# Column sums of all eighth pairs ahead of the second slice, weights rounded later in a block, keys turned one tile later, in a one-core hybrid attention and mLSTM layer

## The chip, the cores and the metric

The kernel runs on one core of a Trainium2 chip. The core's engines work from queues of their own: PE (TensorE, matmuls), DVE (VectorE), ACT (ScalarE), POOL (GpSimd) and SP (SyncE, which here only issues transfers). An instruction waits at the head of its engine's queue until what it needs is there, and what stands behind it in that queue waits too. The metric is device time in microseconds (us); before the change the median of three runs is 1348.02.

## The reference

One layer over 2048 tokens of width 1024, all in float32:

```python
mod = c_act @ w_ada[l] + b_ada[l]
shift, scale, gate = jnp.split(mod, 3, axis=-1)
h = rmsnorm(h_res, norm_w[l]) * (1.0 + scale[:, None, :]) + shift[:, None, :]
y = hybrid_mixer(h, w_in[l], b_in[l], conv_w[l], conv_b[l], rpb[l], ml_norm_w[l], w_out[l])
h_res = h_res + gate[:, None, :] * y
...
def hybrid_mixer(h, w_in, b_in, conv_w, conv_b, rpb, ml_norm_w, w_out):
    proj = h @ w_in + b_in
...
    na_out = neighbourhood_attention(na_q, na_k, na_v, rpb) * jax.nn.silu(na_z)
    qk = jax.nn.silu(centred_short_conv(jnp.concatenate([ml_q, ml_k], axis=-1), conv_w, conv_b))
...
    h_fwd = mlstm_chunkwise(mq, mk, mv, i_f, f_f)
    h_bwd = flip(mlstm_chunkwise(flip(mq), flip(mk), flip(mv), flip(i_b), flip(f_b)))
    hm = (h_fwd + h_bwd).transpose(0, 2, 1, 3) * jax.nn.sigmoid(ml_o).reshape(B, T, ML_HEADS, ML_HEAD_DIM)
...
    return jnp.concatenate([na_out, ml_out], axis=-1) @ w_out
```

`c_act` is silu of the conditioning vector. `proj` is 1024 columns to 4624: queries, keys, values and gate of an attention with 8 heads over a grid of 32 x 64 tokens, the same and one more for an mLSTM with 4 heads that runs in both directions, and 16 columns of mLSTM gates. `centred_short_conv` is a convolution with five taps along the tokens. The last step is another RMSNorm.

## The kernel before

Every float32 matmul of the projection is done in three passes with operands split in a high and a low part: high by high, high by low, low by high. So the 1024 rows that are summed over, eight k-tiles of 128, make 24 matmuls for a tile of output. Each part of the weights has therefore to be "rounded" once it is loaded: ACT copies it to its high half `whi`, another engine subtracts that from the raw weights into the low half `wlo`. `raw_w` (L201) issues the two loads of a block of 256 columns, 512 KB each (`raw0`, `raw1`, one buffer each), and hands back two functions, `parts`, which round a half each when they are called. There are two slots for rounded weights, `wslot` (`_a` and `_b` in the trace), used in turn by even and odd blocks.

Tokens are worked in four groups of 512. `hhi` and `hlo` are the halves of h, turned so that k runs over the partitions, for a group. PSUM is used as four buffers `pp` for results, three `tp` for transposes, and one bank `sp` for everything small.

**The start** (`start`, L218) runs with its instructions in the order in which they are written. The modulation is a sum over eight k-tiles of `w_ada`, loaded in 32 transfers of 256 KB in the order in which they are used. It is worked out for an eighth of the columns of h at a time, two eighths (a pair, `e` from 0 to 3) together. `opened(e)` begins the pair's sum in the `sp` bank with the bias. A k-tile of the table `direct` is added on PE by matmuls one column wide; all others are added up on DVE in `acc` (`summed`, L272). `total(e)` (L283) adds `acc` on PE with a column of ones, and `columns(e)` (L286) has ACT make the scale and shift columns `gT` and `shT` of it. `first_h(k)` (L303) then has ACT write `hhi` and h from the turned x, and hands back the subtraction `hlo` for DVE; the list `early` holds two such subtractions. `vo_first` (L589) is a generator: each `next(first)` issues one slice, that is k-tile k of block 0 for the first four token tiles, 8 matmuls with `hhi` (L598) and 4 with `hlo` (L601). `turned(k)` has PE turn x of k into a `tp` bank, two or three slices ahead. The loop over `e` has two slices in each step; `finish()` in it makes total and columns of the next pair.

**Blocks 0 to 5** are values and output gates, tiles of 128 tokens by 256 columns, 24 matmuls each (`mm3`, L541, lines 544 to 546). `vo_group` and `nav_group` do a group of four tiles: a PSUM buffer each, 24 matmuls, and the eviction by DVE, an addition of the bias into `stvo` or `stv` (L618). `tok_blocks` (L676) goes over blocks 2 to 5 and has the next block's two halves rounded behind groups 0 and 1, with the low half on DVE. From here on the order is set by a scheduler at build time, which goes by estimated costs and by what each instruction depends on; `behind` (L1105) is a dependency of order alone, without a wait. After each tile the loops pull one step of `self.chain`, the mLSTM's gate chain (`gate_chain`, L699): the gates are turned on PE into the `sp` bank, `ps_gi` and then `ps_gf`, DVE copies each out to `wide` (L722, L723), then come Exp, Ln, scans, and the table of decays.

**Blocks 6 to 9** are keys and queries of the mLSTM (`conv_blocks`, L869), with columns on the partitions: tiles `pc` of 128 columns by 512 tokens, 24 matmuls each, in four `pp` buffers. ACT evicts a tile with its bias to `u` (L891, four buffers). `conv_step` then advances all tiles under way by one step of `conv_group` (L917), so that a `yield` in it is one tile later: first nothing, then five taps on DVE into `acc_k` or `acc_q` (four buffers) and a SiLU on ACT (L929), then a store to `d_ck`, and for keys one step later four transposes on PE into `kt` (L939), an eviction `stk` on ACT (L941) and a store.

After that come the queries and keys of the attention (`pq`, L986), the mLSTM's two passes, the attention and the output projection; the change does not touch them.

Of the kernel before, what the change touches and what calls it, by code (L numbers as in the profile page):

```python
# [8 lines left out]
F32 = mybir.dt.float32  # L9
F32R = mybir.dt.float32r  # L10
AF = mybir.ActivationFunctionType
ALU = mybir.AluOpType
# [3 lines left out]
P = 128  # L16
# [4 lines left out]
GT = 512  # L21
# [41 lines left out]
class Kernel:  # L63
# [137 lines left out]
    def raw_w(self, blk, slot, halves=(0, 1)):  # L201
        nc = self.nc
        hi, lo = self.wslot[slot]

        def part(half):
            raw = self.raw.tile([P, 4, 256], F32, tag=f"raw{half}", name=f"raw_{blk}_{half}")
            nc.sync.dma_start(raw, self.w_main[blk, :, 4 * half : 4 * half + 4, :])
            ks = slice(4 * half, 4 * half + 4)

            def run(eng=nc.gpsimd):  # L210
                nc.scalar.activation(hi[:, ks, :256], raw, AF.Copy)
                eng.tensor_tensor(lo[:, ks, :256], raw, hi[:, ks, :256].bitcast(F32), ALU.subtract)

            return run

        return [part(half) for half in halves]

    def start(self, left):  # L218
        nc = self.nc
# [41 lines left out]
        def added(e, left, right):  # L261
            for j in range(4):
                left_tile = left[:, j // 2, (j % 2) * P : (j % 2 + 1) * P]
                groups[e] -= 1
                nc.tensor.matmul(mods[e][:, j : j + 1], left_tile, right, start=False, stop=groups[e] == 0)
# [6 lines left out]
        def summed(e, kt):  # L272
            w, c = sums.pop((e, kt)), cact[:, kt : kt + 1]
            if kt in direct[e]:
                added(e, w, c)
            elif kt == 0:
                acc[e] = ada.tile([P, 2, 256], F32, tag="acc", bufs=2, name=f"acc_{e}")
                nc.vector.tensor_scalar(acc[e], w, c, None, ALU.mult)
            else:
                nc.vector.scalar_tensor_tensor(acc[e], w, c, acc[e], ALU.mult, ALU.add)  # L280
            next(stream, None)

        def total(e):  # L283
            added(e, acc.pop(e), self.ones[:, 0:1])

        def columns(e):  # L286
            ks, ps = slice(2 * e, 2 * e + 2), mods.pop(e)
            for j in range(2):
                k = slice(2 * e + j, 2 * e + j + 1)
                nc.scalar.activation(self.gT[:, k], ps[:, 2 + j : 3 + j], AF.Identity, bias=nw[:, k], scale=nw[:, k])  # L290
            nc.scalar.activation(self.shT[:, ks], ps[:, 0:2], AF.Copy)

        direct = {0: (1, 3), 1: (1,), 2: (1,), 3: (1,)}
        sums, acc, groups = {}, {}, {}
        tps, mods = {}, {}

        def turned(k, tts=(0, 1, 2, 3)):
            if k not in tps:
                tps[k] = self.tp.tile([P, GT], F32, tag="tp", name=f"tp_0_{k}")
            for tt in tts:  # L300
                nc.tensor.transpose(tps[k][:, tt * P : (tt + 1) * P], xt[tt][:, k * P : (k + 1) * P], self.ident)

        def first_h(k):  # L303
            hi = self.hhi[0][:, k, :]
            tp = tps.pop(k)
            h = xp.tile([P, GT], F32, tag="h", bufs=2, name=f"h_0_{k}")
            for dst in (hi, h):
                nc.scalar.activation(dst, tp, AF.Identity, bias=self.shT[:, k : k + 1], scale=self.gT[:, k : k + 1])
            return lambda: nc.vector.tensor_tensor(self.hlo[0][:, k, :], h, hi.bitcast(F32), ALU.subtract)
# [14 lines left out]
        raws = []  # L324
# [22 lines left out]
        hi, lo = self.wslot[0]  # L347
# [34 lines left out]
        for e in range(4):  # L382
            k = 2 * e
            rest = [kt for kt in range(KT) if e < 3 and kt not in direct[e + 1]]
            early = [first_h(k), first_h(k + 1)]
            for n, kt in enumerate(rest[:5]):
                summed(e + 1, kt)
                if n in (2, 4):
                    early.pop(0)()
            for fn in early:  # L390
                fn()
            if e == 1:
                raws[1](nc.vector)
            for kt in rest[5:]:
                summed(e + 1, kt)
            if e == 2:
                for _ in stream:
                    pass
                parts = self.raw_w(1, 1)
                nc.sync.dma_start(self.bgate, self.b_row[0:1, 1536:1552].broadcast_to([P, 16]))  # L400
                self.load_bias(0)
                self.load_bias(1)
                parts[0](nc.vector)

            def finish():
                total(e + 1)
                columns(e + 1)

            next(first)
            if k + 3 < KT:  # L410
                turned(k + 3)
            if e < 3:
                opened(e + 1)
                summed(e + 1, direct[e + 1][0])
            if e == 0:
                finish()
            next(first)
            if k + 4 < KT:
                turned(k + 4)
            if e in (1, 2):  # L420
                finish()
        for tt in range(4, 8):
            load_x(tt)
        parts[1]()
# [147 lines left out]
    def nav_group(self, blk, slot, g):  # L572
        nc = self.nc
        c0 = (blk - 4) * 256
        st = self.stage_tile(f"stv_{blk}_{g}")
        for o in range(4):
            ps = self.pp.tile([P, GT], F32, tag="pp", name=f"pv_{blk}_{g}_{o}")
            self.tok_tile(ps[:, :256], self.wslot[slot], 4 * g + o)
            nc.vector.tensor_add(st[:, o, :256], ps[:, :256], self.brows[blk % 2])
            next(self.chain, None)  # L580
            if o == 1:
                self.flush()
        dst = self.d_vna[g * GT : (g + 1) * GT, c0 : c0 + 256].rearrange("(o p) c -> p o c", p=P)
        self.defer(lambda: nc.sync.dma_start(dst, st[:, :, :256]))
# [91 lines left out]
    def tok_blocks(self, chain_pool):  # L676
        self.wide = chain_pool.tile([P, 2 * D], F32, name="wide")
        self.chain = itertools.chain(self.gate_both(chain_pool), self.decays(chain_pool))
        order = [2, 3, 4, 5]
        next(self.chain)  # L680
        self.tables_begin(chain_pool)
        for n, blk in enumerate(order):
            parts = self.raw_w(blk + 1, (blk + 1) % 2)
            if blk < 5:
                self.load_bias(blk + 1)
            for g in range(NG):
                if blk < 4:
                    self.vo_group(blk, blk % 2, g)
                else:
                    self.nav_group(blk, blk % 2, g)  # L690
                if g < 2:
                    parts[g](self.nc.vector)
            if n > 0:
                self.tables_columns(n - 1)
        for _ in self.chain:
            pass
        self.flush()
# [219 lines left out]
    def conv_group(self, pool, u, kind, ct, g):  # L917

        nc = self.nc
        yield  # L920
        acc = pool.tile([P, GT], F32, tag="acc", bufs=4, name=f"acc_{kind}_{ct}_{g}")
        cc = ct + (0 if kind == "q" else 4)
        for j in range(5):
            src, w = u[:, j : GT + j], self.cw[:, cc, j : j + 1]
            if j == 0:
                nc.vector.tensor_scalar(acc, src, w, None, ALU.mult)
            else:
                nc.vector.scalar_tensor_tensor(acc, src, w, acc, ALU.mult, ALU.add)
        nc.scalar.activation(acc, acc, AF.Silu, bias=self.cb[:, cc : cc + 1])  # L929
        yield  # L930
        j = 0 if kind == "q" else 1
        dst = self.d_ck[ct, 4 * g : 4 * g + 4, :, 385 + j * CH : 385 + (j + 1) * CH].rearrange("c p t -> p c t")
        nc.sync.dma_start(dst, acc.rearrange("p (c t) -> p c t", t=CH))
        yield
        if kind == "q":
            return
        ps = self.tp.tile([P, GT], F32, tag="tp", name=f"kt_{ct}_{g}")
        for o in range(4):
            nc.tensor.transpose(ps[:, o * P : (o + 1) * P], acc[:, o * CH : (o + 1) * CH], self.ident)  # L939
        st = self.stage_tile(f"stk_{ct}_{g}")[:, :, 0:128]  # L940
        nc.scalar.activation(st, ps.rearrange("p (a q) -> p a q", a=4), AF.Copy, scale=KSCALE)  # L941
        d2 = self.d_ck[ct, 4 * g : 4 * g + 4, :, 0:128].rearrange("o p c -> p o c")
        nc.sync.dma_start(d2, st)
# [872 lines left out]
```

## Time and profile before

| | before |
|---|---|
| three runs, us | 1343.64, 1349.42, 1348.02 (median 1348.02) |
| profiled execution, us | 1342.71, of which its span 1340.9 |
| data moved | 255.91 MB, 191 GB/s on the mean |
| start up to the last slice of the first four tiles | 0 to 54 us |
| block 2 begins; key and query blocks | 148 us; 342 to 532 us |
| share of `pq` (L986) in the chain that ended last | 21% |

The profile is of one execution. Its page names groups of instructions by line, engine and tile, output first: `pvo<-whi_a,hhi` is a matmul from `whi_a` and `hhi` into the PSUM tile `pvo`. Behind `<-` in square brackets stands the idle time of the engine before the instruction, and what ended it. In a row of waits the three numbers are the total in us, how many there were, and the longest. In windows each engine has its busy time and, in brackets, its instructions; the granted clock is the share of full speed at which TensorE was allowed to run. Matmuls are pipelined, so the length of one overlaps the next, and the distance between two starts tells more of the pace. The mean granted clock over the whole span is 0.988.

### The profile page before, as it was taken

To read this page: it belongs to the slowest core of one execution; us is meant where nothing else is said; L and a number is where in the kernel's file an instruction comes from. 1 tells how busy PE (TensorE), PEld (TensorE's weight loads), DVE (VectorE), ACT (ScalarE), POOL (GpSimd) and SP (SyncE) were. 2 spreads that over 40 slices of the span, in tenths; PEclk is the share of its full clock that TensorE was granted. 3 is DMA by queue.
4 is the path that set the end of the run, shared out by engine and by line. 5 is a ranking of instruction groups with operands and counts; after the bars stand their busy time and mean duration, and the time that the engine had idled before them with its cause. 6 is when DMAs were issued, how large, how long until landed. Compare 5 with 4: busy or idle time off the path is not lost.

```text
span 1340.9 us, 23409 instructions
## 1 busy us (share of the span) xinstructions
PE 1302.3 (97%) x8330; PEld 1121.7 (84%) x8330; DVE 779.5 (58%) x2404; ACT 543.1 (40%) x1184; POOL 227.0 (17%) x281
## 2 busy tenths in 40 slices
PE   9899899999999999999999999999999999999996
PEld 8899899999877787888888888888877777778785
DVE  5654342212444769256677777777547676766664
ACT  5443323643223423123333323333346555565551
POOL 0144102341000000001212002212202211212221
PEclk8899899999999999999999999999999999999998
DMA  9997545997337775535656867655788987868871
GB/s 321 307 256 182 182 134 156 219 255 217 95 88 216 172 193 163 177 111 141 192 175 191 244 193 212 217 177 169 207 254 226 217 194 189 188 180 192 197 185 48
DMA packets 240486, 255.91 MB, mean 191 GB/s; under 512 B 31078, under 2 KB 200294, under 8 KB 240370
## 3 DMA queue, kind: packets, MB, share of 16 engines
q1 hardware_dynamic: 157006, 182.98, 48.9%
q0 software_dynamic: 20496, 36.21, 11.2%
q10 hardware_dynamic: 62868, 35.22, 9.2%
q8 instruction: 66, 1.08, 0.3%
q14 instruction: 50, 0.41, 0.1%
HBM read 169.81 MB, written 92.72 MB: 196 GB/s over the span
## 4 chain that ended last, share of the span: by engine, by line
PE 48%; DMA 7%; DVE 5%; issue 4%; ACT 2%; POOL 1%; ACTq 0%; SPq 0%; DVEq 0%; POOLq 0%
PE pq L986 21%; PE y L1565 9%; DMA tab<-d_t 4%; PE pT L1505 3%; PE pO L1520 2%; PE pS L1477 2%; PE px L1225 2%; PE pi L1227 2%; PE pc L544 2%; PE pc L546 2%; PE pc L545 2%; PE dc L1165 1%; DMA ck<-d_ck 1%; PE a L1212 1%; DVE pbuf L1485 1%
## 5 line engine op out<-in xcount | busy, mean ns | idle before, releaser
L986 PE MATMUL pq<-hhi,whi_a 128*128 128x512 f32 x512 | 208.2, 407 | 0.8 <-ACT u L891 0.8
L986 PE MATMUL pq<-hlo,whi_a 128*128 128x512 f32 x512 | 208.4, 407 | 0.0
L986 PE MATMUL pq<-hhi,wlo_a 128*128 128x512 f32 x512 | 206.6, 404 | 0.0
L986 PEld LDWEIGHTS pq<-hhi,whi_a 128*128 128x128 f32 x512 | 96.8, 189 | 17.7 <-ACT u L891 1.2
L986 PEld LDWEIGHTS pq<-hhi,wlo_a 128*128 128x128 f32 x512 | 96.8, 189 | 16.4
L986 PEld LDWEIGHTS pq<-hlo,whi_a 128*128 128x128 f32 x512 | 96.7, 189 | 16.0 <-issue 0.5
L1507 ACT ACTIVATE pt<-pT 96x384 f32<-96x384 f32 (+3 forms) x128 | 65.9, 515 | 86.0 <-PE pT L1505 83.4
L960 POOL TENSOR_TENSOR wlo_a<-rawq,whi_a 128x1024 fp32r<-128x1024 f32 x20 | 48.2, 2411 | 306.1 <-ACT whi_a L959 292.7
L1486 ACT ACTIVATE pbuf<-pbuf,mn 128x480 f32<-128x480 f32 (+5 forms) x128 | 76.1, 595 | 51.8 <-DVE mn L1485 49.1
L1565 PE MATMUL y<-hhi,whi_a 128*128 128x512 f32 x256 | 91.6, 420 | 0.5 <-ACT whi_a L1535 0.5
L1565 PE MATMUL y<-hhi,wlo_a 128*128 128x512 f32 (+1 forms) x272 | 90.6, 399 | 0.2 <-ACT y L1572 0.2
L1485 DVE CUSTOM_DVE_ANT_0 pbuf<-pS,tab 128x480 f32<-128x480 f32 (+5 forms) x128 | 63.1, 540 | 38.4 <-PE pS L1477 28.9
L1230 ACT ACTIVATE num<-px,gtile 128x129 f32<-128x129 f32 x120 | 38.3, 366 | 112.7 <-PE px L1225 86.3
L618 DVE TENSOR_TENSOR stvo<-pvo,brow 128x256 f32<-128x256 f32 x64 | 26.7, 422 | 91.9 <-PE pvo L546 68.4
L1505 PEld LDWEIGHTS pT<-ident,pbuf 128*128 128x128 f32 (+2 forms) x416 | 50.8, 137 | 28.8 <-issue 8.9
L1505 PE MATMUL pT<-ident,pbuf 128*128 128x128 f32 (+2 forms) x416 | 67.1, 274 | 7.2 <-DVE pbuf L1497 5.8
L544 PE MATMUL pvo<-whi_b,hhi 128*128 128x256 f32 x256 | 72.9, 285 | 1.1 <-DVE gates L620 1.1
L546 PE MATMUL pvo<-whi_b,hlo 128*128 128x256 f32 x256 | 72.1, 281 | 0.0
L545 PE MATMUL pvo<-wlo_b,hhi 128*128 128x256 f32 x256 | 72.0, 281 | 0.0
L1249 POOL TENSOR_TENSOR hm<-hm,ck 128x128 f32<-128x128 f32 x64 | 26.5, 414 | 254.2 <-DVE hm L1248 223.9
L833 ACT ACTIVATE dec<-dec,gtile 128x128 f32<-128x128 f32 x128 | 42.2, 393 | 41.5 <-POOL dec L826 37.0
L1565 PEld LDWEIGHTS y<-hhi,wlo_a 128*128 128x128 f32 x272 | 48.1, 189 | 9.0 <-issue 2.4
(301 smaller groups left out, 3386.3 us busy)
## 6 DMA issues: line engine op xcount, KB each, us to landing
ck<-d_ck SPq DMA_DIRECT2D x64, 384.5 KB
rawq<-in_w_main_dram SPq DMA_DIRECT2D x28, 512.0 KB
raw<-in_w_main_dram SPq DMA_DIRECT2D x20, 512.0 KB
d_ck<-stvo SPq DMA_DIRECT2D x16, 514.0 KB
kv<-d_ck SPq DMA_DIRECT2D x64, 128.5 KB
wada<-in_w_ada_dram SPq DMA_DIRECT2D x32, 256.0 KB
dec<-d_mneg SPq DMA_DIRECT2D x32, 256.0 KB
d_ck<-dec ACTq DMA_DIRECT2D x32, 256.0 KB
```

The costliest lines, as they stand in the source:

```text
L544: nc.tensor.matmul(ps, lhi(k), rhi(k), start=(k == 0), stop=False)
L545: nc.tensor.matmul(ps, lhi(k), rlo(k), start=False, stop=False)
L546: self.mark = nc.tensor.matmul(ps, llo(k), rhi(k), start=False, stop=(k == KT - 1))
L833: nc.scalar.activation(t[:, o, :], t[:, o, :], AF.Exp, bias=self.cols["g"][:, d, h, c : c + 1])
L960: nc.gpsimd.tensor_tensor(lo[:, :, cs], raw, hi[:, :, cs].bitcast(F32), ALU.subtract)
L986: self.mark = nc.tensor.matmul(patch_ps(ps) if patch else ps, w, self.htok(h, g, k, patch), start=(k == 0 and n == 0), stop=(k == KT - 1 a ...
L1230: nc.scalar.activation(num[:, d, :], px[:, d, :], AF.Copy, scale=self.cols["inter"][:, d, h, c : c + 1])
L1485: nc.vector.tensor_tensor_reduce(pt[:, :nk], ps, tabs[place[u]][j][:, :nk], 1.0, 3e38, ALU.add, ALU.min, mn)
L1486: nc.scalar.activation(pt[:, :nk], pt[:, :nk], AF.Exp, bias=mn, scale=-1.0, accum_out=sums[:, j : j + 1])
L1505: nc.tensor.transpose(ps[:cs, i, :], U[u][j][:, i * cs : (i + 1) * cs], self.ident)
L1507: nc.scalar.activation(t[:cs, :nch, :], ps[:cs, :nch, :], AF.Copy)
L1565: nc.tensor.matmul(y, m[:, k, :], w[k][:, cs], start=(k == 4 and n == 0), stop=(k == 3 and n == 2))
```

## The change

Three parts of the order are changed; no arithmetic is.

- In `start`, `finish()` (total and columns of the next pair) comes ahead of the second slice of the step for all of `e` = 0, 1 and 2; before, for `e` = 1 and 2 it came behind that slice and its turns. To match, all additions to the next pair's sum are made before the first slice; for `e` = 1 the low halves `hlo` stay after the third and fifth of them, as for `e` = 0, and for `e` = 2 they go after the fifth and seventh. The second half of block 0's weights is rounded after the fifth addition of `e` = 1.
- In `tok_blocks` the next block's halves are rounded behind groups 1 and 2 (the second and the third), not 0 and 1. The subtraction of each half is held behind the last eviction written before it, by an order dependency, for blocks 3 and on.
- In `conv_group` a key is turned one tile later (one more `yield`), four tiles behind its own matmuls, and the sums have five buffers where they had four.

```diff
--- before.py
+++ after.py
@@ -209,7 +209,9 @@
 
             def run(eng=nc.gpsimd):
                 nc.scalar.activation(hi[:, ks, :256], raw, AF.Copy)
-                eng.tensor_tensor(lo[:, ks, :256], raw, hi[:, ks, :256].bitcast(F32), ALU.subtract)
+                step = eng.tensor_tensor(lo[:, ks, :256], raw, hi[:, ks, :256].bitcast(F32), ALU.subtract)
+                if blk > 2 and eng is nc.vector:
+                    self.behind(step, self.evicted)
 
             return run
 
@@ -383,16 +385,14 @@
             k = 2 * e
             rest = [kt for kt in range(KT) if e < 3 and kt not in direct[e + 1]]
             early = [first_h(k), first_h(k + 1)]
-            for n, kt in enumerate(rest[:5]):
+            for n, kt in enumerate(rest):
                 summed(e + 1, kt)
-                if n in (2, 4):
+                if n in ((2, 4), (2, 4), (4, 6))[e]:
                     early.pop(0)()
+                if e == 1 and n == 4:
+                    raws[1](nc.vector)
             for fn in early:
                 fn()
-            if e == 1:
-                raws[1](nc.vector)
-            for kt in rest[5:]:
-                summed(e + 1, kt)
             if e == 2:
                 for _ in stream:
                     pass
@@ -412,13 +412,11 @@
             if e < 3:
                 opened(e + 1)
                 summed(e + 1, direct[e + 1][0])
-            if e == 0:
+            if e < 3:
                 finish()
             next(first)
             if k + 4 < KT:
                 turned(k + 4)
-            if e in (1, 2):
-                finish()
         for tt in range(4, 8):
             load_x(tt)
         parts[1]()
@@ -576,7 +574,7 @@
         for o in range(4):
             ps = self.pp.tile([P, GT], F32, tag="pp", name=f"pv_{blk}_{g}_{o}")
             self.tok_tile(ps[:, :256], self.wslot[slot], 4 * g + o)
-            nc.vector.tensor_add(st[:, o, :256], ps[:, :256], self.brows[blk % 2])
+            self.evicted = nc.vector.tensor_add(st[:, o, :256], ps[:, :256], self.brows[blk % 2])
             next(self.chain, None)
             if o == 1:
                 self.flush()
@@ -688,8 +686,8 @@
                     self.vo_group(blk, blk % 2, g)
                 else:
                     self.nav_group(blk, blk % 2, g)
-                if g < 2:
-                    parts[g](self.nc.vector)
+                if g in (1, 2):
+                    parts[g - 1](self.nc.vector)
             if n > 0:
                 self.tables_columns(n - 1)
         for _ in self.chain:
@@ -918,7 +916,7 @@
 
         nc = self.nc
         yield
-        acc = pool.tile([P, GT], F32, tag="acc", bufs=4, name=f"acc_{kind}_{ct}_{g}")
+        acc = pool.tile([P, GT], F32, tag="acc", bufs=5, name=f"acc_{kind}_{ct}_{g}")
         cc = ct + (0 if kind == "q" else 4)
         for j in range(5):
             src, w = u[:, j : GT + j], self.cw[:, cc, j : j + 1]
@@ -934,6 +932,7 @@
         yield
         if kind == "q":
             return
+        yield
         ps = self.tp.tile([P, GT], F32, tag="tp", name=f"kt_{ct}_{g}")
         for o in range(4):
             nc.tensor.transpose(ps[:, o * P : (o + 1) * P], acc[:, o * CH : (o + 1) * CH], self.ident)
```

## The prediction

> **What bounds the kernel now.** I read the page's busy times first, then the waits of PE, then the granted clock in windows, and only then the timelines of the places these name.
>
> ```profile
> span 1340.9 us, 23409 instructions
> ...
> PE 1302.3 (97%) x8330; PEld 1121.7 (84%) x8330; DVE 779.5 (58%) x2404; ACT 543.1 (40%) x1184; POOL 227.0 (17%) x281
> ...
> PE ps_gf L713 <- DVE wide L722: 4.4, 1, 4.4
> PE kt L939 <- ACT acc_k L929: 3.7, 5, 1.4
> PE pvo L598 <- ACT hhi L308: 3.5, 3, 1.6
> PE mod L265 <- DVE acc L280: 1.3, 1, 1.3
> ```
>
> PE is busy 97% of the span and no matmul is added or dropped. A gain can only come out of the 38.6 us in which PE stands still, and out of matmuls that run at a lower clock. The waits (total, times, longest, in us) name the three places that the change touches: the first slices of h, `ps_gf` at the head of block 2, and the key turns `kt`. Windows show what clock follows a pause there (columns: window, length, busy time of PE, PEld, DVE, ACT, POOL, granted clock, DMA share, GB/s):
>
> ```profile
> 40.00:45.00 5.00, 4.88 (x28) 4.88 (x29) 4.16 (x7) 3.02 (x5) 0.00 (x0) 0.66 1.00 351
> ...
> 150.00:160.00 10.00, 5.59 (x36) 5.39 (x35) 3.60 (x7) 5.83 (x7) 0.10 (x1) 0.80 0.72 225
> 410.00:420.00 10.00, 8.63 (x40) 6.71 (x39) 6.25 (x13) 4.61 (x6) 0.00 (x0) 1.00 0.58 204
> ```
>
> At the start and behind `ps_gf` the clock falls, so a pause costs more than its own length; at the key turns it stays at 1.00, and a pause costs what it lasts.
>
> **Part 1: column sums ahead of the second slice.** PE, then DVE and ACT, around the steps e=1 and e=2 (start, length, instruction, idle time before it):
>
> ```profile
> 34.54 0.28 PE L270 MATMUL mod<-bada,ident 128*128 128x4 f32 x2
> ...
> 35.58 0.37 PE L598 MATMUL pvo<-whi_a,hhi 128*128 128x272 f32 x1
> ...
> 37.18 0.60 PE L301 MATMUL tp<-ident,x 128*128 128x128 f32 x4
> 37.61 0.95 PE L265 MATMUL mod<-ones,acc 128*128 128x1 f32 x8
> 40.12 0.60 PE L598 MATMUL pvo<-whi_a,hhi 128*128 128x272 f32 x1 [1.56 <-ACT hhi L308]
> ...
> 42.10 1.11 PE L601 MATMUL pvo<-whi_a,hlo 128*128 128x272 f32 x4
> ...
> 44.69 0.37 PE L598 MATMUL pvo<-whi_a,hhi 128*128 128x272 f32 x1
> ...
> 45.78 0.66 PE L601 MATMUL pvo<-whi_a,hlo 128*128 128x272 f32 x4
> 46.28 0.95 PE L265 MATMUL mod<-ones,acc 128*128 128x1 f32 x8
> 48.78 0.40 PE L598 MATMUL pvo<-whi_a,hhi 128*128 128x272 f32 x1 [1.56 <-ACT hhi L308]
> ...
> 53.03 0.95 PE L601 MATMUL pvo<-whi_a,hlo 128*128 128x272 f32 x4
> ```
>
> ```profile
> 34.53 1.53 DVE L280 SCALAR_TENSOR_TENSOR acc<-wada,cact,acc 128x512 f32<-128x512 f32 x2
> ...
> 40.77 0.69 DVE L309 TENSOR_TENSOR hlo<-h,hhi 128x512 fp32r<-128x512 f32 x1 [2.73 <-ACT h L308]
> ...
> 38.60 0.59 ACT L290 ACTIVATE gT<-mod,nw 128x1 f32<-128x1 f32 x2 [5.61 <-PE mod L265]
> ...
> 39.29 0.78 ACT L308 ACTIVATE hhi<-tp,shT,gT 128x512 fp32r<-128x512 f32 x1
> ```
>
> The chain of a pair is total on PE (37.61), columns on ACT (38.60), hhi (39.29 to 40.07), next slice on PE (40.12): 2.46 from the total's start to the end of hhi, and PE has nothing left to do in it. The change puts a slice behind the total. By starts, a slice at full clock takes 46.28 - 44.69 = 1.6, four turns 37.61 - 37.18 = 0.43, opening a sum with its direct part 35.58 - 34.54 = 1.04, and a total about the 0.9 of the eight direct rows. Total, slice and turns are 2.9, more than the chain's 2.46, so hhi is there in time.
>
> What is late next is the sum itself. For e=1 its last addition ends at 34.53 + 1.53 = 36.06, while PE would reach the total at 35.58: a new wait of 0.5. For e=2 four additions stood behind the hlo that idled 2.73 for ACT; two of them now run ahead of it, and by the same durations the sum ends near 41.3, before PE gets there near 42.1. Followed on from 36.1 by these lengths (0.9, 1.6, 0.43; 1.6, 0.43, 1.04, 0.9, 1.6; then two slices of 1.7), the stage ends near 48.0 instead of 53.98, which is 6.0 less. That is the two pauses (3.1) and two stretches of low clock, less the 0.5. The price of such a stretch: the slice at 40.12 ends at 43.21 (3.1 long), the one at 44.69 at 46.44 (1.75), and its turns add 0.2: 1.5.
>
> On PE's queue, at the step e=1 (`mod_2` is the PSUM tile of the sum, `acc_2` DVE's part of it, `tp_0_5` and `tp_0_6` turned x, `pvo_0` the slices), it stood like this before:
>
> ```order
> L601 MATMUL pvo_0_3_372<-whi_a_124,hlo0_103 128x272
> L301 MATMUL tp_0_6_483<-ident_84,x_0_158 128x128
> L301 MATMUL tp_0_6_483<-ident_84,x_1_160 128x128
> L301 MATMUL tp_0_6_483<-ident_84,x_2_162 128x128
> L301 MATMUL tp_0_6_483<-ident_84,x_3_164 128x128
> L265 MATMUL mod_2_465<-ones_89,acc_2_428 128x1 x4
> L598 MATMUL pvo_0_0_369<-whi_a_124,hhi0_102 128x272
> ```
>
> and with the change:
>
> ```order
> L303 MATMUL tp_0_5_460<-ident_84,x_3_164 128x128
> L272 MATMUL mod_2_465<-bada_154,ident_84 128x4
> L267 MATMUL mod_2_465<-cact_153,wada_2_1_281 128x1 x4
> L267 MATMUL mod_2_465<-ones_89,acc_2_428 128x1 x4
> L596 MATMUL pvo_0_0_369<-whi_a_124,hhi0_102 128x272
> ```
>
> The total now directly follows the opening, one slice and four turns earlier.
>
> Two things may eat from the 6.0. Turns, opening, wait and total now stand together from 34.10 to 37.0 with hardly any long matmul: 2.9 us, as long as the stretch 37.18 to 40.12 that was followed by the low clock. If it drops again, 1.5 is lost. [...] Second, what follows was itself timed by ACT and POOL:
>
> ```profile
> 51.77 2.40 POOL L212 TENSOR_TENSOR wlo_b<-raw,whi_b 128x1024 fp32r<-128x1024 f32 x1 [50.26 <-ACT whi_b L211]
> ```
>
> ACT's last h moves from 50.7 to about 46.5, 4.2 earlier, and this split with it; PE moves 6.0. So the first tile of block 1 may wait some tenths for it. I take **4.5** of the 6.0, with bounds of 1.5 (both low stretches stay and 1.5 more is waited for) and 6.0.
>
> **Part 2: weights rounded two and three groups into the block.** The head of block 2, DVE first, then PE:
>
> ```profile
> 148.42 0.42 DVE L618 TENSOR_TENSOR stvo<-pvo,brow 128x256 f32<-128x256 f32 x1 [2.42 <-PE pvo L546]
> 151.86 1.23 DVE L212 TENSOR_TENSOR wlo_b<-raw,whi_b 128x1024 fp32r<-128x1024 f32 x1 [3.02 <-ACT whi_b L211]
> 154.96 1.23 DVE L212 TENSOR_TENSOR wlo_b<-raw,whi_b 128x1024 fp32r<-128x1024 f32 x1 [1.87 <-ACT whi_b L211]
> 156.10 0.42 DVE L618 TENSOR_TENSOR stvo<-pvo,brow 128x256 f32<-128x256 f32 x1
> 156.43 0.28 DVE L722 COPY wide<-ps_gi 128x128 f32<-128x128 f32 x1
> ...
> 156.77 0.47 PE L713 MATMUL ps_gf<-ident,wide 128*128 128x128 f32 x1 [4.41 <-DVE wide L722]
> ...
> 157.26 0.42 PE L545 MATMUL pvo<-wlo_a,hhi 128*128 128x256 f32 x1
> ...
> 162.97 0.28 PE L545 MATMUL pvo<-wlo_a,hhi 128*128 128x256 f32 x1
> ```
>
> `ps_gf` needs the one PSUM bank that `ps_gi` holds until DVE has copied it. That copy stands behind two splits of block 3's weights, which wait for ACT and a load; everything behind them on DVE waits too, and so does PE. Then the matmuls run at 0.42 instead of 0.28 for 6 us: 28 rows that stand 0.21 apart instead of 0.12, or 2.7 us. Pause and low clock cost 7.1. In DVE's queue at this place (`wlo_b_127` is the low half of block 3's weights), before:
>
> ```order
> L618 TENSOR_TENSOR stvo_1_3_1602<-pvo_1_15_1691,brow1_132 128x2x128
> L212 TENSOR_TENSOR wlo_b_127<-raw_3_0_1750,whi_b_126 128x1024
> L212 TENSOR_TENSOR wlo_b_127<-raw_3_1_1752,whi_b_126 128x1024
> L618 TENSOR_TENSOR stvo_2_0_1755<-pvo_2_0_1757,brow0_131 128x2x128
> L722 COPY wide_1724<-ps_gi_1783 128x128
> L723 COPY wide_1724<-ps_gf_1786 128x128
> ```
>
> and now:
>
> ```order
> L616 TENSOR_TENSOR stvo_1_3_1602<-pvo_1_14_1663,brow1_132 128x2x128
> L616 TENSOR_TENSOR stvo_1_3_1602<-pvo_1_15_1691,brow1_132 128x2x128
> L616 TENSOR_TENSOR stvo_2_0_1755<-pvo_2_0_1757,brow0_131 128x2x128
> L720 COPY wide_1724<-ps_gi_1783 128x128
> L721 COPY wide_1724<-ps_gf_1786 128x128
> ```
>
> Both splits have left this place. One eviction interval after 148.42 (0.42 + 2.42) the first tile of block 2 is evicted, to 151.7, and the copy ends near 151.9; PE comes to `ps_gf` near 152.0, two matmuls earlier than before. I subtract 0.2 and take **6.9**; bounds 3 (the copy is late by 3 for a reason not seen here, at low clock) and 7.1.
>
> The five pairs of splits that move are costed at nothing. Each is 1.23 on DVE between evictions 2.84 apart, with four PSUM tiles before PE would feel it. The second half comes four tiles, 11.4 us, before its block ends, and needs 2.3 on ACT and DVE. The loads of the next block are issued a group or two later on SP's queue, since the buffer is freed later, but still more than two groups before their use. If that cover were gone, see the last rival.
>
> **Part 3: keys turned four tiles behind, five sum buffers.**
>
> ```profile
> 415.30 0.66 PE L939 MATMUL kt<-ident,acc_k 128*128 128x128 f32 x4 [1.37 <-ACT acc_k L929]
> ...
> 467.87 0.65 PE L939 MATMUL kt<-ident,acc_k 128*128 128x128 f32 x4 [1.30 <-ACT acc_k L929]
> ...
> 382.71 0.69 ACT L891 ACTIVATE u<-pc,bcol 128x512 f32<-128x512 f32 x1 [5.32 <-PE pc L546]
> ...
> 450.41 0.60 ACT L941 ACTIVATE stk<-kt 128x512 f32<-128x512 f32 x1 [10.08 <-PE kt L939]
> ...
> 433.31 0.49 DVE L926 TENSOR_SCALAR acc_k<-u,cw 128x512 f32<-128x512 f32 x1 [4.74 <-DMA d_ck<-acc_k]
> ```
>
> A tile takes 5.32 + 0.69 = 6.0, and the longest wait for a key's SiLU is 1.37: one tile later the SiLU is long done. The fifth buffer also lets DVE start a sum while an older one is still being stored (the 4.74). I take the whole **3.7**; bounds 0 and 4.5 (PE also waits 0.8 once for ACT u at the end of the convolution).
>
> **The sum.** 4.5 + 6.9 + 3.7 = 15.1. The profiled execution took 1342.71 us, 1.8 more than its span; less 15.1 it is 1327.6. The median of the three runs shown, 1348.02, lies 5.3 above it, and less 15.1 gives 1332.9. I state **1332 us**.
>
> **Rivals.**
> 1. *The start gives nearly nothing*: the low clock stays and ACT's chain is next. For it: 2.9 us without long matmuls, clocks of 0.66. Against: hhi comes ahead of PE by the lengths above. Price 4.5 - 1.5 = 3: 1336.
> 2. *ACT's queue in the convolution becomes the bound.* ACT already stood 10.08 before 450.41, with the evictions `u` of later tiles queued behind a `stk` whose turn PE had not reached. One tile more makes it 16. PE has four PSUM tiles, 24 us, so I expect no stall; if they run out, 6 us more and a low clock (2.7) take 9 of the gain: 1341 to 1342, about no change.
> 3. *The pause at `ps_gf` only moves on*, to the Exp and Ln that feed the next step. It would keep the 7: 1340. Against it: the next PE step that needs them is three tiles later.
> 4. *Slower: weights late.* The second half is ready only after its block has ended, at five block heads, each with the low clock behind it (2.7). It exceeds the gain of 15.1 by 0.5% when each pause is over 1.7 (5 x 4.4 = 22): 1348 + 7 = 1355. It decides from a split that is 9.1 us late (11.4 - 2.3). For it: the loads move back on SP. Against: the loads take about 7, by
>
> ```profile
> 404.30 2.26 SPq L207 DMA_DIRECT2D raw<-in_w_main_dram x2
> ...
> 411.33 1.06 ACT L211 ACTIVATE whi_a<-raw 128x1024 fp32r<-128x1024 f32 x1 [3.73 <-DMA raw<-in_w_main_dram]
> ```
>
> and have more than two groups, 22 us.
>
> **Chances.** Forecast 0.63, rival 1 0.14, rival 2 0.08, rival 3 0.05, rival 4 0.10. Half a per cent, 6.7 us, is about what a measurement of this kernel can tell from no change: faster means below 1341.3. Faster: forecast, rival 1 and two hundredths of rivals 2 and 3, 0.79; same: the rest of these, 0.11; slower: rival 4, 0.10. The bounds of the terms (4.5 to 17.6) give 1330 to 1343 on the median's scale and 5 less on that of the profiled run. Runs of one kernel differ by 5.8 here, so I put the range at 1322 to 1342, which leaves out rival 4 and the edge of rival 2.
>
> **What would show it.** In the changed profile: the second slice of e=1 follows a total with at most 0.5 of waiting, and the third and fourth slices' 1.56 are gone; the stage ends near 48 to 50; the clock of 25 to 30 stays low, since e=0 is as it was. `ps_gf` waits under 0.5, and 150 to 160 has a clock of 1.00. The wait `kt` on `acc_k` is under 1 in total. Wrong would be: a new wait of PE for `whi` or `wlo` at a block's head, for `u` in the convolution, or a second drop of the clock at 36 to 43 that costs more than 1.5.

## The result, and the profile after

The changed kernel takes 1330.57 us (median of 4 runs, 1328.03 to 1332.39) against 1348.09 (4 runs, 1343.64 to 1349.42): a ratio of 0.9874, interval 0.9846 to 0.9902, which is 13 to 21 us. Forecast were 1332 and a range of 1322 to 1342. The profiled execution took 1330.81, so on its own scale the gain is 11.9 (1342.71 - 1330.81), where 15.1 were forecast. The page of the changed kernel (its line numbers differ by one or two):

```profile
span 1329.0 us, 23407 instructions
...
PE 1297.6 (98%) x8330; PEld 1118.7 (84%) x8330; DVE 780.1 (59%) x2404; ACT 543.4 (41%) x1184; POOL 228.7 (17%) x281
```

PE's waits, in the columns of the prediction:

```profile
PE pq L985 <- ACT u L889: 3.7, 1, 3.7
...
PE kt L938 <- ACT acc_k L927: 1.4, 1, 1.4
...
PE pvo L596 <- ACT hhi L310: 0.4, 1, 0.4
```

`ps_gf` (4.4) is gone, `hhi` fell from 3.5 to 0.4, and `kt` from 3.7 to 1.4. New is 3.7 at the first `pq`, where 0.8 stood before. The windows at the places of the prediction:

```profile
30.00:35.00 5.00, 5.00 (x26) 5.00 (x25) 4.75 (x8) 3.35 (x5) 0.00 (x0) 0.54 1.10 348
35.00:40.00 5.00, 5.00 (x37) 4.99 (x36) 4.82 (x8) 2.38 (x6) 0.00 (x0) 0.81 1.07 356
40.00:45.00 5.00, 5.00 (x39) 5.00 (x38) 3.73 (x5) 2.00 (x3) 0.00 (x0) 0.85 1.01 358
...
150.00:160.00 10.00, 10.00 (x85) 9.59 (x84) 6.65 (x19) 6.01 (x8) 0.10 (x1) 1.00 0.48 119
```

Behind `ps_gf` the clock is full now (1.00, 0.80 before). Between 30 and 45 PE no longer stands still, but it runs two stretches at a low clock (0.54, 0.81 and 0.85 in the three windows). In PE's timeline the second of them begins in the slice behind the moved total, with no pause ahead:

```profile
36.49 1.05 PE L267 MATMUL mod<-ones,acc 128*128 128x1 f32 x8
37.40 0.37 PE L596 MATMUL pvo<-whi_a,hhi 128*128 128x272 f32 x1
...
38.16 0.43 PE L596 MATMUL pvo<-wlo_a,hhi 128*128 128x272 f32 x1
...
41.28 0.38 PE L596 MATMUL pvo<-wlo_a,hhi 128*128 128x272 f32 x1
41.49 0.29 PE L596 MATMUL pvo<-whi_a,hhi 128*128 128x272 f32 x1
...
50.56 0.36 PE L542 MATMUL pvo<-whi_b,hhi 128*128 128x256 f32 x1 [0.32 <-DVE gates L618]
```

Block 1 begins at 50.56 instead of 54.16. How the stages compare over all profiled executions is best seen in one table. It is worked out from first starts on PE (of `whi_b` in `pvo`, of `pc`, of `pq`) and the span; "waits" are PE's at `kt` and at the first `pq`, and DVE's longest for a turned key.

| kernel | start to block 1 | blocks 1 to 5 | keys and queries | rest | waits kt, pq, DVE | ratio to before (interval) |
|---|---|---|---|---|---|---|
| before | 54.2 | 288.0 | 191.2 | 807.5 | 3.7, 0.8, 0 | 1 |
| changed | 50.6 | 280.8 | 190.9 | 806.7 | 1.4, 3.7, 11.8 | 0.9874 (0.9846 to 0.9902) |
| e1 start only | 48.6 | 291.5 | 195.1 | 807.0 | 4.8, 0.8, 0 | 0.9969 (0.9948 to 0.9991) |
| e2 blocks only | 54.6 | 282.8 | 191.3 | 808.7 | 3.7, 0.8, 0 | 0.9924 (0.9898 to 0.9950) |
| e3 keys only | 54.3 | 291.4 | 193.0 | 809.5 | 2.0, 5.0, 9.0 | 0.9994 (0.9974 to 1.0014) |
| e4 keys undone | 50.5 | 281.3 | 195.7 | 807.5 | 6.4, 0.8, 0 | 0.9898 (0.9869 to 0.9926) |
| e5 changed again | 48.4 | 282.7 | 192.7 | 807.2 | 1.2, 5.6, 10.2 | 0.9884 (0.9853 to 0.9914) |
| e6 u first | 50.5 | 282.5 | 189.8 | 807.1 | 1.1, 2.9, 10.3 | 0.9880 (0.9851 to 0.9909) |
| e7 turns placed | 49.1 | 282.0 | 195.1 | 806.3 | 6.0, 0.8, 0 | 0.9911 (0.9881 to 0.9941) |
| e8 filled pause | 51.9 | 282.0 | 192.8 | 816.5 | 1.9, 5.1, 9.5 | 0.9957 (0.9936 to 0.9979) |
| e9 turns soon | 48.9 | 281.0 | 192.8 | 805.8 | 3.4, 0.8, 0.9 | 0.9880 (0.9854 to 0.9906) |
| e10 more dense | 49.8 | 282.8 | 193.1 | 819.4 | 2.0, 3.7, 10.0 | 0.9970 (0.9951 to 0.9988) |
| e11 halves, soon | 49.3 | 281.4 | 186.7 | 805.9 | 0.2, 0.8, 0 | 0.9844 (0.9821 to 0.9868) |
| e12 halves | 50.0 | 281.4 | 186.7 | 805.4 | 0.1, 0.8, 0 | 0.9858 (0.9830 to 0.9886) |

### The profile page after: what moved, and what is told of

Its sections match the earlier page's. It is cut to its first block, busy times and chain, and to the rows that moved or that the text cites. A ratio compares the mean times of both kernels' runs of the same rounds, so it can differ in the third digit from the quotient of the medians.

```text
span 1329.0 us, 23407 instructions
## 1 busy us (share of the span) xinstructions
PE 1297.6 (98%) x8330; PEld 1118.7 (84%) x8330; DVE 780.1 (59%) x2404; ACT 543.4 (41%) x1184; POOL 228.7 (17%) x281
## 4 chain that ended last, share of the span: by engine, by line
PE 74%; DMA 8%; DVE 7%; issue 7%; ACT 1%; SPq 1%; POOL 1%; DVEq 0%; POOLq 0%; ACTq 0%
PE pq L985 18%; PE y L1564 11%; PE pvo L542 4%; PE pvo L544 3%; PE pvo L543 3%; DMA tab<-d_t 3%; PE pc L542 3%; PE pc L544 3%; PE pT L1504 3%; PE pc L543 3%; PE pO L1519 2%; PE pvo L596 2%; PE pv L544 2%; PE pv L543 2%; PE pv L542 2%
## 5 line engine op out<-in xcount | busy, mean ns | idle before, releaser
L959 POOL TENSOR_TENSOR wlo_a<-rawq,whi_a 128x1024 fp32r<-128x1024 f32 x20 | 48.4, 2419 | 301.4 <-ACT whi_a L958 250.5
L577 DVE TENSOR_TENSOR stv<-pv,brow 128x256 f32<-128x256 f32 x32 | 13.0, 423 | 72.8 <-PE pv L544 43.5
```

The costliest lines, as they stand in the source:

```text
L959: nc.gpsimd.tensor_tensor(lo[:, :, cs], raw, hi[:, :, cs].bitcast(F32), ALU.subtract)
```

## Experiments

**The three parts, each alone, and the keys undone** (e1 to e4, on one chip). Each applies the hunks of its part of the change to the kernel before; e4 takes the keys' hunks out of the changed kernel.

e1, in `start`, with the additions of the sums moved to match:

```diff
-            if e == 0:
+            if e < 3:
                 finish()
...
-            if e in (1, 2):
-                finish()
```

e2, in `tok_blocks`, with the subtraction held behind the last eviction:

```diff
-                if g < 2:
-                    parts[g](self.nc.vector)
+                if g in (1, 2):
+                    parts[g - 1](self.nc.vector)
```

e3, in `conv_group`, which e4 undoes:

```diff
-        acc = pool.tile([P, GT], F32, tag="acc", bufs=4, name=f"acc_{kind}_{ct}_{g}")
+        acc = pool.tile([P, GT], F32, tag="acc", bufs=5, name=f"acc_{kind}_{ct}_{g}")
...
+        yield
         ps = self.tp.tile([P, GT], F32, tag="tp", name=f"kt_{ct}_{g}")
```

> The kernel before with the change of the start alone. Theory: the two pauses of 1.56 before hhi go, one stretch of low clock stays behind the new run of short matmuls; block 1's first tile begins 3.6 to 4.3 us earlier, near 50 instead of 54.16, and the end moves by the same 3.6 to 4.3 (ratio about 0.997). Rival: a start that ends earlier is given back at ps_gf or at the later loads, and the end moves by under 1 us. Both: ps_gf still waits 4.4 for DVE's copy, and kt still waits about 3.7 in total.

> The kernel before with the later rounding of weights in the token blocks alone. Theory: ps_gf's wait of 4.4 and the low clock behind it go, nothing else moves: the first pc matmul comes 7.2 us earlier than before's 342.2, and the end moves by 7 (ratio about 0.9947). Rival: part of the gain in the changed kernel's blocks came from the earlier start (loads that land earlier); then this alone brings under 5. A late half of weights would show as a PE wait for whi or wlo at a block's head; none is expected.

> The kernel before with the later turn of the keys and the fifth sum buffer alone. Theory: the waits of kt fall from 3.7 to about 1.4, but DVE idles some 12 us for a key's turn, comes later to the last SiLUs, and the last u, queued behind one of them on ACT, makes the first pq wait about 3.7 with a low clock behind it; from the first pc to the first pq it takes 190.9 against 191.2 before, and with the low clock after it the end is 0 to 2 us later than before (ratio 1.000 to 1.0015). Rival: the wait of the first pq is a chance of one execution; then this alone brings 2 to 3.7 us (ratio about 0.998).

> The changed kernel with the part on the keys undone. Theory: as fast as the changed kernel or 0 to 2 us faster (1328.5 to 1331 where that has 1330.6): kt waits 3.7 again, the first pq waits only 0.8. Rival, that the part on the keys brings what was forecast: 3 to 4 us slower than the changed kernel, 1334.

Measured: the start alone 0.9969 (4.2 us by 1348.2, interval 1.2 to 7.0), the blocks alone 0.9924 (10.2, 6.7 to 13.8), the keys alone 0.9994 (0.8, -1.9 to 3.5). They add up to 15.2. Undoing the keys gave 0.9898, slower than the changed kernel rather than as fast, but the two intervals overlap; the keys are worth somewhere between nothing and 3 us. Part of the spread lies in the old order of the keys. PE's order in this stage is the same in the kernel before, e1, e2 and e4, yet the stage took 191.2 and 191.3 in before and e2, and 195.1 and 195.7 in e1 and e4. There one turn waited 2.87 and 3.02, where the longest wait had been 1.37, and in e1 the clock was low from 465.96 to 472.79.

```profile
466.91 1.12 PE L935 MATMUL kt<-ident,acc_k 128*128 128x128 f32 x4 [2.87 <-ACT acc_k L925]
```

Whether that is chance or comes with the earlier start, which e1 and e4 share, stays open.

The surprise is e2, 10.2 where 7 were expected. Its own blocks are 282.8 long, near the changed kernel's 280.8, but e1 and e3, which keep the old blocks, took 291.5 and 291.4 there and not the 288.0 of the profile of before. PE's waits in e1 have a row that this profile lacks:

```profile
PE pv L540 <- DVE stv L575: 3.3, 1, 3.3
```

DVE's timeline shows where it is from. This is e1, in block 5:

```profile
289.59 0.42 DVE L575 TENSOR_TENSOR stv<-pv,brow 128x256 f32<-128x256 f32 x1 [2.42 <-PE pv L542]
301.94 1.93 DVE L212 TENSOR_TENSOR wlo_a<-raw,whi_a 128x1024 fp32r<-128x1024 f32 x1 [11.92 <-ACT whi_a L211]
```

and this the same place of the kernel before, as profiled:

```profile
296.82 0.43 DVE L579 TENSOR_TENSOR stv<-pv,brow 128x256 f32<-128x256 f32 x1 [2.42 <-PE pv L546]
304.41 1.23 DVE L212 TENSOR_TENSOR wlo_a<-raw,whi_a 128x1024 fp32r<-128x1024 f32 x1 [7.16 <-ACT whi_a L211]
```

Block 6's split held back the evictions of block 5 in both, because ACT's rounding stood in its queue behind the table of decays. For 7.16 PE had PSUM tiles left; for 11.92 it ran out of them and stood 3.3, with a low clock in e1's window:

```profile
300.00:310.00 10.00, 6.69 (x43) 6.49 (x43) 5.57 (x7) 6.87 (x17) 5.70 (x3) 0.83 1.02 274
```

So the old blocks have a second pause of the kind at `ps_gf`, present in e1 and e3 and absent in the one execution of the kernel before that was profiled. The change removes it too. What is left in the new blocks is smaller: in e2 and e5 PE waits 1.4 and 1.5 at `pv`, where DVE stands up to 11.7 before a buffer whose store is late.

**The changed kernel again, and three edits to it** (e5 to e8, on one chip).

e6 holds the last three SiLUs behind the last `u`:

```diff
+                    self.last_u = nc.scalar.activation(u[:, 2 : GT + 2], ps, AF.Identity, bias=bias)
...
+        late = 4 * ct + g - 10 if kind == "q" else 0
+        for _ in range({1: 3, 2: 2, 3: 1}.get(late, 0)):
+            yield
...
+        if late > 0:
+            self.behind(silu, self.last_u)
```

e7, in `mm3`, holds the next tile's first matmul behind the turns written before it:

```diff
+            for turn in self.key_turns:
+                self.behind(first, turn)
+            self.key_turns = []
```

e8, in `finish`:

```diff
+                for i in range(8 if e == 0 else 0):
+                    nc.tensor.matmul(self.firsts[0][:, 272:512], hi[:, i % 4, :P], hi[:, i % 4, :240], start=False, stop=False)
                 total(e + 1)
```

> The changed kernel as it is, for comparison on the same chip and for a second profile. Theory: the wait of the first pq for u comes back at 3 to 5 us, since DVE again idles over 10 us for a key's turn near the end of block 7; ratio 0.985 to 0.990. Rival: that wait was a chance of one execution and is under 1.5 here.

> The changed kernel with the last u (tile 9_1_3) ahead of the SiLUs of the last tiles on ACT, which are held behind it. Theory: the first pq waits 0.8 instead of 3.7 and no low clock follows: 2.9 and 2.0 less, 4.9 us in all, ratio to before about 0.984 where the changed kernel has 0.9874. Rival: what follows is bound by DVE, which has the same sums left, and gives it back: under 1.5 us. DVE's idle time of 12 us for the turn stays in both.

> The changed kernel with each key's turn held on PE at the place where it is written, between two pc tiles, so that the three turns that stood together behind 8_0_2 come one, two and three tiles earlier. Theory: ACT's wait of 15.6 before stk and DVE's of 11.8 before the sum that needs the turned buffer go, DVE comes to the end of the convolution up to 10 us earlier, the last SiLUs with it, and the first pq waits under 1 without any change of order there: 4 to 5 us less than the changed kernel. Rival: DVE then waits for stores of the sums or for u in the same places and is as late at the end; the wait of the first pq stays over 3 and the time is that of the changed kernel.

> The changed kernel with eight matmuls of 240 columns, into columns that nothing reads, in the pause of 1.29 ahead of the total of e=0. Theory: it is the pause that is followed by the low clock; filled, the stretch that ran from 28.75 to 34.96 at 0.23 us per matmul runs at 0.12, and block 1 begins 2.5 to 3 us earlier. Rival: turns, openings and totals, short matmuls, make for the low clock whether PE pauses or not (so it was at 38 to 41, with no pause): the low clock stays and the time is the same or up to 1 us longer.

e5: the wait of the first `pq` came back, at 5.6, and so did DVE's for a turn, at 10.2. Over all kernels the two go together: every one in which DVE waited 9 to 12 for a turned key has 2.9 to 5.6 at the first `pq`, all others have 0.8. How the wait travels is seen in the changed kernel's own timelines. PE (its order puts the turns of keys 2_1, 2_2 and 2_3 together behind tile 8_0_2):

```profile
441.25 1.47 PE L938 MATMUL kt<-ident,acc_k 128*128 128x128 f32 x12
...
522.28 0.51 PE L985 MATMUL pq<-hhi,whi_a 128*128 128x512 f32 x1 [3.70 <-ACT u L889]
...
522.93 0.63 PE L985 MATMUL pq<-hhi,wlo_a 128*128 128x512 f32 x1
```

DVE, whose next sum needs a buffer that is free only when its key is turned:

```profile
441.89 0.49 DVE L924 TENSOR_SCALAR acc_k<-u,cw 128x512 f32<-128x512 f32 x1 [11.80 <-PE kt L938]
```

and ACT, there and at the end of the queries:

```profile
441.94 0.60 ACT L940 ACTIVATE stk<-kt 128x512 f32<-128x512 f32 x1 [15.63 <-PE kt L938]
...
520.93 0.72 ACT L927 ACTIVATE acc_q<-acc_q,cb 128x512 f32<-128x512 f32 x1 [1.25 <-DVE u L893]
521.56 0.67 ACT L889 ACTIVATE u<-pc,bcol 128x512 f32<-128x512 f32 x1
```

There is one more link between the two places. DVE catches up after 442 and idles again. But the sum that had waited 11.80 comes to its SiLU only at 452.87, and five sums later the next one in turn for the same buffer waits for its store:

```profile
478.77 0.49 DVE L924 TENSOR_SCALAR acc_q<-u,cw 128x512 f32<-128x512 f32 x1 [9.39 <-DMA d_ck<-acc_k]
```

From there DVE works with hardly a pause and is still behind at the end. Its last sum begins 9.2 after that tile's matmuls; in all six profiles in which DVE waited 9 to 12 for a turn it is 9.2 to 11.1, in the other eight 4.1 to 6.2. The last `u` stands behind a SiLU that waits for DVE, and `pq` needs the PSUM that this `u` frees.

e6 shows that the order on ACT at the end is not the cause: with `u` ahead of those SiLUs it waited 3.70 for DVE itself, since its own buffer was still being summed from, and the time was that of e5 (0.9880 against 0.9884). The rival held. e7 confirms the first half of the theory: with the turns in their place neither ACT nor DVE waits for one, and the first `pq` waits 0.8. But PE pays for it, in one piece:

```profile
419.25 1.12 PE L942 MATMUL kt<-ident,acc_k 128*128 128x128 f32 x4 [6.04 <-ACT stk L945]
```

The turn found no PSUM tile, because the `stk` that empties one was waiting for a stage buffer whose store was still running. e7 is no faster than e5, its median 4 us longer.

e8: filled, the first pause was followed by a full clock, as expected; but block 1 began at 51.9, later and not earlier, and the kernel was slower, 0.9957. The windows:

```profile
25.00:30.00 5.00, 4.67 (x39) 4.48 (x40) 3.24 (x6) 1.65 (x5) 0.00 (x0) 1.00 1.09 350
30.00:35.00 5.00, 3.54 (x29) 3.24 (x27) 4.93 (x8) 2.74 (x4) 0.00 (x0) 1.00 1.10 348
35.00:40.00 5.00, 3.79 (x18) 3.79 (x19) 4.53 (x7) 2.05 (x6) 0.00 (x0) 0.65 1.06 363
```

PE only came sooner to the next total, and waited there, with the low clock behind that pause instead:

```profile
36.21 1.67 PE L267 MATMUL mod<-ones,acc 128*128 128x1 f32 x8 [2.42 <-DVE acc L282]
```

DVE's timeline shows what set the time of that total:

```profile
29.38 1.54 DVE L282 SCALAR_TENSOR_TENSOR acc<-wada,cact,acc 128x512 f32<-128x512 f32 x2 [1.02 <-DMA wada<-in_w_ada_dram]
...
34.63 1.53 DVE L282 SCALAR_TENSOR_TENSOR acc<-wada,cact,acc 128x512 f32<-128x512 f32 x2
```

DVE waited for its last late load until 29.38 and then worked without a pause to the end of the sum. In the changed kernel it was the same 29.38 and the total started at 36.49, in e5 28.66 and 35.53. So the total comes some 7 us after that load, whatever the clock on PE did before. Up to the first `pq` e8 lost 3 us against e5 and 4 against the changed kernel; the rest comes behind it (last section).

**The turns a tile late, and four places for their stage** (e9 and e10 on one chip, e11 and e12 on another).

e9, in `mm3`, holds a turn at most one tile behind its place:

```diff
+            if k == 0:
+                for turn in self.turns_due:
+                    self.behind(first, turn)
+                self.turns_due, self.key_turns = self.key_turns, []
```

e10, in `start`:

```diff
-        filler(6)
+        filler(14)
```

e12, in `conv_group`; e11 has e9's edit as well:

```diff
-        st = self.stage_tile(f"stk_{ct}_{g}")[:, :, 0:128]
+        if g % 2 == 0:
+            self.key_stage = self.stage_tile(f"stk_{ct}_{g}")
+        st = self.key_stage[:, :, 128 * (g % 2) : 128 * (g % 2) + 128]
```

> The changed kernel with each key's turn held on PE no later than one tile behind its written place, so that 2_1, 2_2 and 2_3 come behind 7_1_2, within 7_1_3 and behind 7_1_3 instead of together behind 8_0_2. Theory: the PSUM buffer that PE waited 6.0 for with the turns in their written place is free by then (the stk that freed it ran at 418.6, one tile ahead), so kt waits under 2 in total; DVE no longer waits 10 for a turn, the first pq waits 0.8 instead of 3.7 to 5.6, and no low clock follows it: 187 to 189 us from the first pc to the first pq and a ratio to before of 0.984 to 0.986, 3 to 6 us less than the changed kernel. Rival: the stores that free the stk buffers set the pace of the turns wherever they stand, PE waits 4 to 6 at one of them, and the time is that of the kernel with the turns in their written place, ratio 0.990 to 0.992.

> The changed kernel with eight more matmuls of 256 columns into the unused tile dense, behind the turns of the third slice, where the start already has six: the same number of added PE instructions as in the filled pause, none of them in its place. Theory, that the 8 to 10 us which the filled pause lost behind the first pq came with its own late start of block 1 and its chance waits: this kernel takes 0.5 to 1.5 us more than the changed one and needs 807 from the first pq to the end, ratio 0.987 to 0.990. Rival: any eight more instructions ahead make all that follows on PE slower: over 812 from the first pq to the end, ratio over 0.993.

> The kernel with the turns at most one tile late, and two keys sharing the two halves of a stage buffer (four places for stk where there were two), so that every second stk waits for no store. Theory: ACT's waits for stores of stk were what PE waited 3.4 for at the turns; they fall from 20 to under 12, kt waits under 1.5, the first pq 0.8, and from the first pc to the first pq it takes 188 to 190 against 190.9 to 192.8: 2 to 4 us less than the changed kernel, ratio 0.984 to 0.987. Rival: the stores themselves take the time, both halves are only free when the later store is done, and ACT waits as long at every second stk: 192 or more, ratio 0.988 or more.

> The changed kernel with two keys sharing a stage buffer, and no other hold on the turns (PE's order then puts 2_1 and 2_2 behind 7_1_1 and 7_1_2, and 2_3 still behind 8_0_2). Theory: the stk buffers are why the changed kernel's turns were put three tiles late; DVE's wait for a turn falls from 10 to under 5, the first pq's from 3.7 to 5.6 to under 2.5; 0 to 3 us less than the changed kernel, ratio 0.985 to 0.988. Rival: the turn of 2_3, still two tiles late, holds DVE and ACT as before: the first pq waits over 3 and the ratio is 0.988 or more.

e9 fell between the two: the first `pq` waits 0.8, but PE waits 3.4 for `stk` at two turns, and 192.8 us and 0.9880 are the changed kernel's. So wherever the turns stand, something waits for the stage buffers: ACT for stores of `stk` by the waits of the changed kernel (27.4 in total in the kernel before)

```profile
ACT stk L940 <- DMA d_ck<-stk: 27.0, 9, 8.2
```

and of e11

```profile
ACT stk L948 <- DMA d_ck<-stk: 7.1, 3, 2.8
```

With two keys in one buffer that fell to a quarter. PE then waits 0.2 at the turns, DVE not at all for one, and the stage of keys and queries takes 186.7, 4.4 less than before. e12, without a hold on the turns, does it in 186.7 as well. There ACT still stood 14.2 for a turn, but DVE did not, and the first `pq` waited 0.8: so it is DVE's wait that goes on to `pq`, not ACT's. e11 has the lowest ratio here, 0.9844, 1328.51 us on its chip against 1350.35. Its interval and that of e5 overlap a little, so that it beats the changed kernel rests on the lengths of the stage (186.7 in both against 190.9 to 193.1 in five profiles with the keys as changed). ACT waited for this one kind of store nine times in the changed kernel, and three times when the places were doubled.

## Why the prediction was right, and where it was not

- *The start, 4.5.* Over all profiles with its edit and no added matmul, block 1 begins at 48.4 to 50.6, 49.5 on the mean of nine, against 54.2 to 54.6 without it: 4.8, and 4.2 by time for e1. The steps were met in the main: hhi was there in time (0.4 waited), and the wait for the sum, forecast at 0.5, was 0.6 in e1 and between nothing (the changed kernel) and 2.4 (e9) elsewhere. The second drop of the clock behind the short matmuls came in three of the nine (the changed kernel, e4 and e6); there block 1 begins at 50.5 to 50.6, in the other six at 49.0 on the mean. The difference is the 1.5 that the prediction named for it.
- *The head of block 2, 6.9.* The pause and its low clock are gone. The term was too small because of the other splits, which the prediction costed at nothing "with four PSUM tiles before PE would feel it". Only one of three profiles with the old blocks kept that margin: in e1 one split held DVE for 11.9, in e3 for 12.8, and PE stood still a second time. Blocks 1 to 5 took 290.3 on the mean of these three and 281.9 with the edit, 8.4 less (10.2 by time).
- *The keys, 3.7.* Here the step "I take the whole 3.7" failed. The waits at `kt` went but for 1.4 (under 1 was expected), and the gain was spent at the first `pq`. That is a new wait for `u` at the end of the convolution, which the prediction had named as a sign of being wrong. The stage took 192.5 on the mean of five profiles against 193.3 on the mean of four without, 0.8 less. The size is uncertain: e3 is 1.7 longer than before and e2, while the changed kernel, e5, e8 and e10 are 3.0 shorter than e1 and e4, which start as early. So the reading that a pause at a turn costs only what it lasts, at a clock of 1.00, held for one execution and not for e1 and e4 (1.1 and 2.7 more of waits at `kt` than before, the stage 3.9 and 4.5 longer). The mechanism was half seen. Rival 2 had ACT stand 16 us before a `stk` (it was 15.63), and asked whether PE's four PSUM tiles would last. They did. What was not asked is who else waits for a turn: DVE, whose sum buffers are freed by it. A fifth buffer was read as relief for a wait for stores (4.74). That wait went, a wait of 11.80 for PE came, and the wait for a store returned five sums later, at 9.39.
- *The sum.* On the stage lengths the change is worth 4.8 + 8.4 + 0.8 = 14.0, near the 15.1 forecast; 17.5 was measured, with an interval of 13 to 21. The prediction added the distance of the profiled run from the median, 5.3, as if it were chance alone; by the 288.0 against 291.4 and 291.5, some 3.4 of it is likely the second pause, which that execution lacked. This error and the one at the keys went opposite ways. That 1332 came so near is in part luck.
- *The rivals.* Weights were not late: PE waits for no `whi` or `wlo` in blocks 2 to 6. The pause at `ps_gf` did not move on. Of rival 1 the low clock came true in three of nine profiles, not its price.

## What to carry to other kernels

A profile is one execution: a wait that used up most of its cover there (7.2 of 11.4 us) was a pause in others (11.9 in e1, 12.8 in e3), so a margin should be priced by how much it can vary and not set to nothing. When an operation is put later, ask of every buffer it frees who takes that buffer next, on all engines; three edits to the order only moved the wait, until the buffer at its root, two stage tiles whose stores ACT waited for, was given more places. And where another engine sets the pace, as DVE does with the sums of the start, filling a pause of PE only lengthened the next (2.42 in e8, 1.02 in e5).

## What the runs showed that was not expected

Eight matmuls more in the start, in either of two places, made the kernel slower by some 10 us: e10 has 0.9970 and e8 0.9957, against 0.9884 for the same kernel without them. So the rival of e10 held, that eight more instructions ahead slow down what follows. Up to the first `pq` they lose 2 to 4; the rest takes 819.4 in e10 and 816.5 in e8 instead of the 805.4 to 809.5 of all twelve other profiles. In e10 the loss shows at the two changes of head in the mLSTM, as waits for loads with a low clock behind them:

```profile
766.00:796.00 30.00, 27.02 (x135) 21.60 (x134) 19.63 (x72) 6.20 (x17) 0.41 (x1) 0.94 0.60 175
...
826.00:856.00 30.00, 27.60 (x147) 23.47 (x146) 20.41 (x88) 11.38 (x27) 7.24 (x8) 0.94 0.64 200
```

In the changed kernel the clock is 1.00 at both places. e8 loses 2 and 3 at the same two, and 4 more near 1166. The order of the instructions on PE, the eight matmuls apart, and on DVE, ACT and POOL is the same in both as in the changed kernel. Why so small an addition so early tells there stays open.

The low clock came in stretches of two lengths. The granted clock that the profiles record was low in e5 from 28.51 to 31.92, in the changed kernel from 38.05 to 41.47 (0.50 on the mean of 38.1 to 41.4), and in e8 from 36.46 to 43.28: 3.41, 3.41 and 6.83 long. All other stretches in the fourteen profiles have one of these two lengths, but for the last, which runs past the end of the work. The same instructions gave one single stretch in e5, and a double and a single one in the changed kernel (27.81 to 34.64, 38.05 to 41.47), and that goes with the difference between 48.4 and 50.6. Pauses of 1.29 (e5) and 2.42 (e8) were followed by one, and so was, in the changed kernel, a run of short matmuls without any pause (34.96 to 37.40). What sets where a stretch falls, and its length, the runs do not show.
